# Attention values: full products for the low halves of a head's first queries, and V's largest magnitude taken by halves

## The chip, the cores and the metric

The kernel runs on one core of a Trainium2 chip. The core has a matrix engine (TensorE, PE in the profile; its weight loads are listed apart as PEld), a vector engine (VectorE, DVE), an activation engine (ScalarE, ACT), GpSimd (POOL) and SyncE (SP), whose queue issues the DMA transfers here. Each engine takes its own instructions in the order in which the program has them and waits on semaphores for the others. Operands lie in SBUF, the products' sums in PSUM, which has eight banks of 128 partitions by 512 numbers.

The metric is the device time of one execution in microseconds. A lower time is better.

## What is computed

Two decoder layers over 1024 tokens of width 1024. Layer 0 mixes by causal pooling, layer 1 by a forgetting attention with 16 heads of 64; both have a second, gated branch that attends to 256 memory tokens. The change lies in layer 1:

```python
def shared_kv(x, w_kv_shared, b_forget):
    h = x @ w_kv_shared
    k = h[..., :D_MAIN].reshape(B, S, FOX_HEADS, FOX_HEAD_DIM)
    v = h[..., D_MAIN:2 * D_MAIN].reshape(B, S, FOX_HEADS, FOX_HEAD_DIM)
    log_f = jax.nn.log_sigmoid(h[..., 2 * D_MAIN:] + b_forget)
    return k, v, jnp.cumsum(log_f, axis=1)

def block(args):                                  # 128 queries of forgetting_attention
    logits = jnp.einsum('bqhd,bkhd->bhqk', qi, k) * FOX_HEAD_DIM ** -0.5
    logits = logits + (ci[..., :, None] - cum_k[:, :, None, :])
    logits = jnp.where(mask[None, None], logits, -jnp.inf)       # causal
    p = jax.nn.softmax(logits, axis=-1)
    return jnp.einsum('bhqk,bkhd->bqhd', p, v)
```

## The kernel before

**Precision by halves.** Inputs are float32. An operand is split into a high and a low part, and a product is summed from high x high, low x high and high x low. The attention's probabilities and values are split into two float16 numbers each: `values_of` scales a pair's V by a power of two and `scaled_halves` writes the high half on ACT (L339) and the low half on DVE (L340). The scale comes from the largest magnitude in each of V's 128 rows: L332 reduces 1024 tokens on DVE to one number, L333 keeps it from being zero, L334 to L337 make the scale and its inverse out of its exponent.

**The forgetting attention, `fox`.** It goes through heads `hd` 0 to 15, two to a pair (`pr`), and in a head through eight tiles of 128 queries, from the last (tile 7, 1024 keys) to the first (tile 0, 128 keys). `probs` makes a tile's logits in one or two parts of up to 512 keys, each in one of three L banks (two products, L231). DVE adds the forget gates' row R, takes the row's minimum (the logits are held negated) and empties the bank in one instruction (L986; R was masked on POOL, L978); the second part starts from the first part's minimum. ACT then takes the exponentials into two T banks with the row sums beside them (L994). DVE adds the sums and inverts them (L1004 or L1006, L1007), and a tile later `halves` writes the scaled probabilities as float16 halves, ACT the high one (L1015) and DVE the low one (L1016). A DMA transposes them (L1028).

**`values(hd, c)`.** Once the four tiles of a half of the queries are transposed, PE multiplies them with V: `c = 1` for tiles 7 to 4 (26 blocks of 128 keys), `c = 0` for tiles 3 to 0 (10 blocks). It sums in one bank, O. In L1045 the stationary side is V's high and low half next to each other, 128 columns, so one product gives high V x high P in partitions 0 to 63 and low V x high P in 64 to 127. In L1051 high V alone, 64 columns, meets the low half of P, and blocks go by turns into the upper and the lower half of the array's columns (`128*64` in the profile). At the end ACT and DVE add both halves of the partitions (L1057, L1058).

**Work in between.** While DVE and ACT make the probabilities, PE works through projections in the order of a list (`Fill`): keys, values and queries of the pair after the next, and gates. They go into two pj banks (L253), 24 products of 128x512 a bank and 48 for both halves of the tokens. `chained` sets a pair's order: keys 48, values 24, queries 48, values 24. Each full bank is emptied by ACT and DVE: keys L893 and L894, queries L904 and L905, gates L283 and L284, values by one ACT copy alone (L931) into a tile `u[0]` of 128x1024. When a pair's projections are through, `complete` calls `values_of` on it. The first two pairs get their V in another way (`v_first`), so that `values_of` runs for six.

The order on PE is that of the code. On the other engines a scheduler sets it from its own estimate of times, so an edit can move instructions that it does not name.

Of the kernel before, what the change touches and what calls it, by code (L numbers as in the profile page):

```python
# [9 lines left out]
F32 = mybir.dt.float32  # L10
# [5 lines left out]
ALU = mybir.AluOpType  # L16
AX = mybir.AxisListType

P = 128
# [80 lines left out]
def trunk_kernel(ctx, tc, x, xT, memT, win, wk, wv0, wv, wmk, wmv, wout, poolw, pscale, lng, lnb, bforget, out):  # L100
# [225 lines left out]

    def scaled_halves(u, halves, un, by_tile=lambda t: t):

        m, e, sc = (tiny(1) for _ in range(3))
        nc.vector.tensor_reduce(m, u, AX.X, ALU.max, apply_absolute_value=True)  # L332
        nc.vector.tensor_scalar(m, m, 2.0 ** -100, None, ALU.max)  # L333
        nc.vector.tensor_scalar(e.bitcast(I32), m.bitcast(I32), 0x7F800000, None, ALU.bitwise_and)  # L334
        nc.vector.reciprocal(sc, e)
        nc.vector.tensor_scalar(sc, sc, 2.0 ** 14, None, ALU.mult)
        nc.vector.tensor_scalar(un, e, 2.0 ** -15 / PSCALE, None, ALU.mult)  # L337
        (hi, lo), u = halves, by_tile(u)
        nc.scalar.activation(hi, u, AF.Copy, scale=sc)  # L339
        nc.vector.scalar_tensor_tensor(lo, u, sc, hi, ALU.mult, ALU.subtract)  # L340
# [415 lines left out]
    with tc.tile_pool(name="in1", bufs=1) as in1:  # L756
# [21 lines left out]

        def values_of(u):

            un = unscale[:, len(done) : len(done) + 1]
            done.append(0)
            two = MK([P, ST, 2, P], F16)
            scaled_halves(
                u, [two[:, :, e, :] for e in range(2)], un, lambda t: t.rearrange("p (s t) -> p s t", s=ST),
            )
            v = vt([P, 2, 2 * ST, 64], F16)
            for b in range(2):
                nc.sync.dma_start_transpose(v[:, b, :, :], two[64 * b : 64 * b + 64].rearrange("p s e t -> p (s e t)"))
            return v, un  # L790
# [95 lines left out]
        def pair_units(p):  # L886
# [41 lines left out]
            if p < 2:  # L928
                return keys, queries
            vals = landing(  # L930
                slab(wv[p - 2], XH, XL, lambda cols, acc: nc.scalar.copy(u[0][:, cols], acc)), u, lambda: [MK([P, S], F32)],  # L931
            )
            return chained((keys, 48), (vals, 24), (queries, 48), (vals, 24))

        def complete(p):
            heads, u = pairs[p]
            pairs[p] = list(heads)
            pairs[p].append(first_vs[p] if p < 2 else values_of(u[0]))

# [94 lines left out]
        def values(hd, c, o):  # L1034
# [9 lines left out]
            for n, (i, j) in enumerate(blocks):  # L1044
# [3 lines left out]
                )  # L1048
            for n, (i, j) in enumerate(blocks):
                half = slice(64 * (n % 2), 64 * (n % 2) + 64)  # L1050
# [203 lines left out]
```

## Time and profile before

| what | value |
|---|---|
| median of 3 runs | 1199.49 us (1198.8 to 1199.53) |
| the profiled execution's own time | 1198.79 us |
| its span, first to last instruction | 1197.0 us |
| mean granted TensorE clock | 0.999 |
| layer 1's attention (`fox`), about | 640 to 1075 us |
| PE busy in 640 to 760, 760 to 820, 820 to 860 us | 116.27, 59.17, 38.39 us |
| PE busy in 860 to 925, 925 to 1015, 1015 to 1060 us | 64.07, 86.69, 44.38 us |

A row of the timeline or of the groups names the line of the kernel, the engine, the operation, output and inputs by the program's tile names, and the shapes. A timeline row begins with its start and duration in us and ends, where the engine stood idle before, with that time and what ended it. A group row has the count, the busy time in us, the mean ns of one, and the idle time before. A row of waits has who waited for whom, us in total, how often, and the longest. A row of the windows has the stretch and its length, then the busy time and count on PE and PEld, the granted clock, the share of the DMA engines and GB/s. "issue" is time for which the profile names no releaser.

### The profile page before, as it was taken

What the parts mean: (1) busy time and instruction counts of PE and PEld (TensorE: products, weight loads), DVE (VectorE), ACT (ScalarE), POOL (GpSimd) and SP (SyncE); (2) the same over time, 40 slices, a digit from 0 to 9 for tenths busy, and PEclk for the clock granted to TensorE, in tenths of its full rate; (3) what the DMA queues carried; (4) which work ended last, traced back from release to release, by engine and by line L of the source; (5) the groups of instructions that cost most, each with busy time, mean ns of one, the idle gap of its engine ahead of it and who ended that gap; (6) DMA issues with size and microseconds to landing.
All of it is one profiled execution on the core that took longest, in us unless ns stands there. A gap on an engine that the chain in (4) does not pass through costs nothing. (4 is left out here: it accounts for less than half of the span.)

```text
span 1197.0 us, 19472 instructions
## 1 busy us (share of the span) xinstructions
PE 1172.2 (98%) x6810; PEld 739.3 (62%) x6927; DVE 800.5 (67%) x1864; ACT 616.9 (52%) x1330; POOL 208.4 (17%) x312
## 2 busy tenths in 40 slices
PE   9999999999999999999999999999999999999997
PEld 4567665555555555677776666666666666655554
DVE  6544767374656576377546888778878888874654
ACT  7433654262532224366325777767766787773110
POOL 2000000000000000200103334333334324530000
PEclk9999999999999999999999999999999999999999
DMA  7333654242355666355526789879897999976431
GB/s 246 115 101 87 131 115 159 79 123 80 102 197 158 159 156 161 106 138 100 171 54 161 152 199 173 195 155 195 187 186 164 195 191 210 230 206 229 154 116 48
DMA packets 280803, 182.06 MB, mean 152 GB/s; under 512 B 225024, under 2 KB 238976, under 8 KB 280704
## 3 DMA queue, kind: packets, MB, share of 16 engines
q1 hardware_dynamic: 280704, 180.81, 62.0%
q8 instruction: 54, 0.88, 0.3%
q14 instruction: 45, 0.37, 0.1%
HBM read 95.24 MB, written 22.61 MB: 98 GB/s over the span
## 5 line engine op out<-in xcount | busy, mean ns | idle before, releaser
L253 PE MATMUL pj<-A,w 128*128 128x512 bf16 (+1 forms) x1817 | 571.4, 398 | 2.2 <-DVE B L894 1.1
L253 PE MATMUL pj<-A,wl 128*128 128x512 bf16 x929 | 351.8, 380 | 6.4 <-issue 3.4
L253 PEld LDWEIGHTS pj<-A,w 128*128 128x128 f32 x944 | 174.8, 188 | 45.4 <-POOL wl L200 2.0
L253 PEld LDWEIGHTS <-w 128*128 128x128 bf16 x960 | 93.1, 98 | 121.3 <-issue 39.4
L253 PEld LDWEIGHTS <-wl 128*128 128x128 bf16 x960 | 94.3, 98 | 87.9 <-issue 4.2
L994 ACT ACTIVATE T<-MK,s 128x512 f32<-128x512 f32 x192 | 111.0, 578 | 44.5 <-DVE s L986 22.6
L1015 ACT ACTIVATE P<-T,s 128x512 f16<-128x512 f32 x192 | 103.1, 576 | 52.8 <-issue 26.3
L1016 DVE SCALAR_TENSOR_TENSOR P<-T,s,P 128x512 f16<-128x512 f32 x192 | 112.3, 612 | 24.0 <-ACT P L1015 22.3
L540 PEld LDWEIGHTS <-T 128*128 128x128 bf16 x736 | 70.6, 98 | 88.9 <-issue 6.8
L190 DVE TENSOR_TENSOR wl<-raw,w 128x512 bf16<-128x512 f32 (+1 forms) x96 | 67.9, 713 | 72.3 <-ACT w L189 69.7
L231 PE MATMUL L<-B,B 128*128 128x512 f32 (+3 forms) x384 | 109.0, 386 | 4.6 <-DVE s L986 4.2
L189 ACT CAST w<-raw 128x512 fp32r<-128x512 f32 (+1 forms) x104 | 62.8, 609 | 84.0 <-PE pj L253 57.6
L231 PEld LDWEIGHTS L<-B,B 128*128 128x128 f32 x384 | 71.1, 189 | 29.6 <-DVE s L986 9.9
L353 POOL TENSOR_SCALAR A<-A 128x1024 bf16<-128x1024 f32 x8 | 8.4, 1049 | 444.5 <-ACT A L351 427.9
L986 DVE CUSTOM_DVE_ANT_0 MK<-L,R 128x512 f32<-128x512 f32 (+3 forms) x128 | 72.8, 569 | 8.4 <-PE L L231 5.6
L978 POOL TENSOR_SCALAR_AFFINE_SELECT R<-R 128x128 f32<-128x128 f32 x128 | 42.2, 335 | 207.4 <-DVE s L986 162.5
L200 POOL TENSOR_TENSOR wl<-raw,w 128x512 bf16<-128x512 f32 x54 | 69.4, 1285 | 3.8
L190 DVE TENSOR_TENSOR T<-T,T 128x1024 bf16<-128x1024 f32 x23 | 31.6, 1374 | 48.1 <-ACT T L189 48.0
L189 ACT CAST T<-T 128x1024 fp32r<-128x1024 f32 x23 | 24.1, 1047 | 71.7 <-DMA T<-y1d 45.4
L199 POOL TENSOR_SCALAR w<-raw 128x512 fp32r<-128x512 f32 x54 | 35.9, 665 | 58.5 <-PE pj L253 58.5
L540 PE MATMUL L<-B,T 128*128 128x512 bf16 (+1 forms) x163 | 43.1, 391 | 0.3
L433 ACT ACTIVATE P<-L,s 128x256 f32<-128x256 f32 x64 | 29.6, 474 | 23.4 <-issue 13.0
(296 smaller groups left out, 1789.7 us busy)
## 6 DMA issues: line engine op xcount, KB each, us to landing
raw<-in_win_dram SPq DMA_DIRECT2D x94, 256.0 KB, 2.9
raw<-in_wout_dram SPq DMA_DIRECT2D x40, 256.0 KB, 2.9
B<-B SPq DMA_DIRECT2D x32, 256.0 KB, 4.5
R<-cumd SPq DMA_DIRECT2D x16, 512.0 KB, 4.6
T<-y0d SPq DMA_DIRECT2D x12, 512.0 KB, 5.1
y0d<-Y SPq DMA_DIRECT2D x11, 512.0 KB, 2.7
T<-y1d SPq DMA_DIRECT2D x11, 512.0 KB, 4.7
raw<-in_wmk_dram SPq DMA_DIRECT2D x16, 256.0 KB, 2.7
```

Of the source, the lines that this page charges most:

```text
L189: pin(nc.scalar.copy(hi, src))
L190: pin(by.tensor_tensor(lo[0], src, hi.bitcast(F32), ALU.subtract))
L199: nc.gpsimd.tensor_scalar(hi, src, 1.0, 1.0, ALU.mult, ALU.mult)
L200: nc.gpsimd.tensor_tensor(lo[0], src, hi.bitcast(F32), ALU.subtract)
L231: nc.tensor.matmul(acc, a, b, start=i == 0, stop=i == len(terms) - 1)
L253: nc.tensor.matmul(acc, a, b, start=start, stop=stop)
L540: nc.tensor.matmul(acc, y, w, start=c == 2 and j == firsts[id(acc)] and acc is not self.seeded, stop=c == 1 and j == lasts[id(acc)], skip_ ...
L978: nc.gpsimd.affine_select(R[:, qs], R[:, qs], [[-1, P]], ALU.is_ge, -NEG, base=0, channel_multiplier=1).ins
L986: nc.vector.tensor_tensor_reduce(p[:, lo:up], lg, R[:, lo:up], 1.0, top, ALU.add, ALU.min, m[:, n : n + 1])
L994: nc.scalar.activation(e, p[:, lo:up], AF.Exp, bias=top, scale=-1.0, accum_out=sums[:, n, hd % 2, i : i + 1],)
L1015: nc.scalar.activation(pair[:, lo:up], e, AF.Copy, scale=r)
L1016: nc.vector.scalar_tensor_tensor(pair[:, L + lo : L + up], e, r, pair[:, lo:up], ALU.mult, ALU.subtract)
```

## The change

In `values`, for `c == 0` only, the low half of P meets V's high and low half together, as in L1045, so that ten products of 64 columns become ten of 128 (and low V x low P is added too). For `c == 1` the code is as before. The second part takes V's largest magnitude per half of the tokens: as soon as ACT has copied a half from its bank, DVE reduces these 512 tokens into one column of a small tile `tops`, and `scaled_halves` takes the larger of the two columns where it took a maximum over 1024 tokens.

```diff
-    def scaled_halves(u, halves, un, by_tile=lambda t: t):
+    def scaled_halves(u, halves, un, by_tile=lambda t: t, tops=None):
         m, e, sc = (tiny(1) for _ in range(3))
-        nc.vector.tensor_reduce(m, u, AX.X, ALU.max, apply_absolute_value=True)
-        nc.vector.tensor_scalar(m, m, 2.0 ** -100, None, ALU.max)
+        if tops is None:
+            nc.vector.tensor_reduce(m, u, AX.X, ALU.max, apply_absolute_value=True)
+            nc.vector.tensor_scalar(m, m, 2.0 ** -100, None, ALU.max)
+        else:
+            nc.vector.tensor_scalar(m, tops[:, 0:1], tops[:, 1:2], 2.0 ** -100, ALU.max, ALU.max)
...
+            def v_evac(cols, acc):
+                nc.scalar.copy(u[0][:, cols], acc)
+                n = cols.start // NH
+                nc.vector.tensor_reduce(u[1][:, n : n + 1], u[0][:, cols], AX.X, ALU.max, apply_absolute_value=True)
+
             vals = landing(
-                slab(wv[p - 2], XH, XL, lambda cols, acc: nc.scalar.copy(u[0][:, cols], acc)), u, lambda: [MK([P, S], F32)],
+                slab(wv[p - 2], XH, XL, v_evac), u,
+                lambda: [MK([P, S], F32), small.tile([P, 2], F32, tag="tops", name=nm("tops"), bufs=2)],
             )
...
-            pairs[p].append(first_vs[p] if p < 2 else values_of(u[0]))
+            pairs[p].append(first_vs[p] if p < 2 else values_of(*u))
...
-            for n, (i, j) in enumerate(blocks):
+            if c == 0:
+                for n, (i, j) in enumerate(blocks):
+                    nc.tensor.matmul(
+                        acc[:, cols(i)], v[:, b, 2 * j : 2 * j + 2, :].rearrange("p e d -> p (e d)"),
+                        pt[hd, i][:, i + 1 + j, :], start=False, stop=n == len(blocks) - 1, skip_group_check=True,
+                    )
+            for n, (i, j) in enumerate(blocks if c else ()):
                 half = slice(64 * (n % 2), 64 * (n % 2) + 64)
                 nc.tensor.matmul(
                     acc[half, cols(i)], v[:, b, 2 * j, :], pt[hd, i][:, i + 1 + j, :],
```

Line numbers behind the edits are higher in the changed kernel: L986, L1004, L1007 and L1016 become L996, L1014, L1017 and L1026.

On PE nothing changes its place. The end of the first `values(hd, 0)`, before:

```order
L1051 MATMUL O_6682<-T_6345,V_6084 64x128
L1051 LDWEIGHTS V_6084
L1051 MATMUL O_6682<-T_6376,V_6084 64x128
L253 LDWEIGHTS w_6410
L253 MATMUL pj_6617<-A_3076,w_6410 128x512
L253 LDWEIGHTS wl_6411
```

and now:

```order
L1061 MATMUL O_6682<-T_6345,V_6084 128x128
L1061 LDWEIGHTS V_6084
L1061 MATMUL O_6682<-T_6376,V_6084 128x128
L253 LDWEIGHTS w_6410
L253 MATMUL pj_6617<-A_3076,w_6410 128x512
L253 LDWEIGHTS wl_6411
```

The rows of L1051 have become rows of the new L1061 with 128 columns, and the same projection stands behind them.

On DVE, in head 3 (whose tiles go on while pair 2's first half of V is copied, MK_7111), from the low halves of an earlier tile to the inverse for tile 7, before:

```order
L1016 SCALAR_TENSOR_TENSOR P_7178<-T_7144,s_7175,P_7178 128x256
L986 ISA MK_7196,s_7200<-L_7208,R_6941,s_7200 128x512
L986 ISA s_7200 128x1
L1016 SCALAR_TENSOR_TENSOR P_7212<-T_7181,s_7205,P_7212 128x128
L1004 TENSOR_SCALAR s_7244<-sums_6812 128x1
L986 ISA MK_7235,s_7239<-L_7240,R_6941 128x512
L986 ISA s_7239 128x1
L1007 RECIPROCAL s_7244<-s_7244 128x1
```

and now:

```order
L1026 SCALAR_TENSOR_TENSOR P_7179<-T_7145,s_7176,P_7179 128x256
L937 TENSOR_REDUCE tops_7112<-MK_7111 128x1
L996 ISA MK_7198,s_7202<-L_7210,R_6941,s_7202 128x512
L996 ISA s_7202 128x1
L1026 SCALAR_TENSOR_TENSOR P_7214<-T_7182,s_7207,P_7214 128x128
L996 ISA MK_7237,s_7241<-L_7242,R_6941 128x512
L996 ISA s_7241 128x1
L1014 TENSOR_SCALAR s_7246<-sums_6812 128x1
L996 ISA MK_7237,s_7241<-L_7249,R_6941,s_7241 128x384
L996 ISA s_7241 128x1
L1017 RECIPROCAL s_7246<-s_7246 128x1
```

The reduce of the first half (L937) stands ahead of the second minimum of tile 7; the first minimum of the next tile has gone ahead of L1014, and its second one ahead of L1017.

On DVE, between heads 3 and 4, where `values_of` runs for pair 2, before:

```order
L332 TENSOR_REDUCE s_7556<-MK_7111 128x1
L333 TENSOR_SCALAR s_7556<-s_7556 128x1
L334 TENSOR_SCALAR s_7557<-s_7556 128x1
L335 RECIPROCAL s_7558<-s_7557 128x1
L337 TENSOR_SCALAR unscale<-s_7557 128x1
L1006 TENSOR_SCALAR s_7582<-sums_6812 128x1
L336 TENSOR_SCALAR s_7558<-s_7558 128x1
L1007 RECIPROCAL s_7582<-s_7582 128x1
L986 ISA MK_7573,s_7577<-L_7578,R_7322 128x512
```

and now:

```order
L937 TENSOR_REDUCE tops_7112<-MK_7111 128x1
L336 TENSOR_SCALAR s_7559<-tops_7112 128x1
L337 TENSOR_SCALAR s_7560<-s_7559 128x1
L338 RECIPROCAL s_7561<-s_7560 128x1
L340 TENSOR_SCALAR unscale<-s_7560 128x1
L1016 TENSOR_SCALAR s_7584<-sums_6812 128x1
L339 TENSOR_SCALAR s_7561<-s_7561 128x1
L1017 RECIPROCAL s_7584<-s_7584 128x1
L996 ISA MK_7575,s_7579<-L_7580,R_7324 128x512
```

The place and the count of rows are the same; L937 reduces the second half alone, where L332 reduced both.

More of the change, by code (lines that the diff above doesn't have):

```diff
@@ L777, in trunk_kernel, with values_of @@
             nc.gpsimd.affine_select(later, later, [[1, P]], ALU.not_equal, 1.0, base=-k * HEADS, channel_multiplier=-1)
-        def values_of(u):
+        def values_of(u, tops):
             un = unscale[:, len(done) : len(done) + 1]
@@ L784, in values_of @@
             scaled_halves(
-                u, [two[:, :, e, :] for e in range(2)], un, lambda t: t.rearrange("p (s t) -> p s t", s=ST),
+                u, [two[:, :, e, :] for e in range(2)], un, lambda t: t.rearrange("p (s t) -> p s t", s=ST), tops,
             )
```

## Prediction

> **What bounds the kernel now.** I read the page first, then the groups by line with shapes kept apart, then the waits of TensorE (PE) and of VectorE (DVE) in stretches of the forgetting-attention stage (about 640 to 1060 us), and last the timeline around single calls.
>
> ```profile
> span 1197.0 us, 19472 instructions
> PE 1172.2 (98%) x6810; PEld 739.3 (62%) x6927; DVE 800.5 (67%) x1864; ACT 616.9 (52%) x1330; POOL 208.4 (17%) x312
> PE L L231 <- DVE s L986: 4.2, 9, 1.0
> PE pj L253 <- issue: 3.8, 24, 0.2
> PE pj L253 <- DVE B L894: 1.1, 2, 0.5
> PE pj L253 <- POOL R L978: 0.3, 2, 0.2
> PE pj L253 <- POOL R L1083: 0.2, 1, 0.2
> ```
>
> The last five rows are PE's waits between 640 and 1075 us, but for one of 0.3 us. PE is busy 98% of the span, so a change pays if it takes PE time away or ends one of its waits. Three kinds of wait matter: nine times (4.2 us) PE waits until the row minimum of L986 has emptied one of the three L banks; twice (1.1 us) until L894 has emptied a pj bank; and 24 times it stands for 0.16 us with no releaser ("issue"). The three waits put down to POOL are as long as those and, like them, stand right behind a call of `values`, so I take them for the same thing.
>
> Whether a saving on PE reaches the end depends on who leads. These are DVE's waits, first in 660 to 763 us (six rows), then the one kind in 764 to 805 us that names PE's logits:
>
> ```profile
> DVE P L1016 <- ACT P L1015: 5.7, 10, 1.1
> DVE s L1004 <- ACT T L994: 5.0, 6, 1.3
> DVE s L1006 <- ACT T L994: 1.7, 5, 0.5
> DVE G L1058 <- ACT G L1057: 1.5, 3, 0.9
> DVE MK L986 <- DVE s L986: 0.3, 2, 0.2
> DVE MK L986 <- PE O L1051: 0.2, 1, 0.2
> ...
> DVE MK L986 <- PE L L231: 0.7, 2, 0.4
> ```
>
> From 660 to 763 us DVE never waits for logits: it waits for ScalarE (ACT), ACT for it, and the two set their own pace, with PE running into the full banks. Only after 764 us does DVE wait for PE. The same answers for 805 to 860 and 910 to 1015 us name no logits, that for 860 to 910 us does. So PE leads in some heads and the DVE-ACT chain in the others.
>
> **Full products in `values(hd, 0)`.** One call, the first of sixteen, on PE:
>
> ```profile
> 673.70 0.72 PE L1045 MATMUL O<-T,V 128*128 128x128 f16 x10
> 674.36 0.47 PE L1051 MATMUL O<-T,V 128*64 128x128 f16 x10
> 674.99 0.38 PE L253 MATMUL pj<-A,wl 128*128 128x512 bf16 x1 [0.16 <-issue]
> ```
>
> From the first full product to the projection behind the call: 674.99 - 673.70 = 1.29 us. Ten full ones, then ten half-array ones that run in pairs, then a stand of 0.16 us. The change makes the ten halves full. What a run of full f16 products costs, its exit into the same kind of projection included, stands in the memory attention:
>
> ```profile
> 151.96 0.84 PE L231 MATMUL T<-T,MK 128*128 128x128 f16 x12
> 152.64 0.38 PE L253 MATMUL pj<-A,w 128*128 128x512 bf16 x1
> ```
>
> Twelve products in 0.68 us, 0.057 each, and no stand behind them. Twenty would take 1.13 us, 0.16 less than now. The last call differs, since another product follows it:
>
> ```profile
> 1068.55 0.73 PE L1045 MATMUL O<-T,V 128*128 128x128 f16 x10
> 1069.21 0.47 PE L1051 MATMUL O<-T,V 128*64 128x128 f16 x10
> 1069.61 0.50 PE L540 MATMUL pj<-MK,B 128*128 128x512 f32 x1
> ```
>
> 1.06 us without a stand; it becomes 1.13, so 0.07 longer. Gross: 15 x 0.16 - 0.07 = 2.3 us less on PE. No instruction is added: 320 rows (a weight load and a product each) change shape, and the weights that they load are the pair of halves that L1045 loads already.
>
> A page speaks against this edit. The Trainium skill, "TensorEngine Tiling (Array Packing)", section Theoretical Speedup, promises up to twofold for a stationary side of 64 columns, which is L1051's case; by that alone the halves are the form to keep, and the sum would be that of the second rival below. The same page, section Key Properties, says that a change of the tiling mode drains TensorE, without a price; the stand of 0.16 us behind the halves agrees with it, and for ten products the trace has the drain dearer than the gain.
>
> How much arrives: a call's 0.16 us is lost where PE next runs into the DVE-ACT chain, because it then waits that much longer. I count as kept the calls after which DVE waits for PE, or no such wait of PE follows:
>
> ```profile
> 751.60:753.00 1.40, 0.47 (x10) 0.31 (x10) 1.00 0.91 180
> 780.70:782.10 1.40, 0.47 (x10) 0.31 (x10) 1.00 0.67 207
> 859.50:860.90 1.40, 0.47 (x10) 0.31 (x10) 1.00 0.95 200
> 888.50:889.90 1.40, 0.47 (x10) 0.31 (x10) 1.00 0.88 237
> 1016.20:1017.70 1.50, 0.47 (x10) 0.31 (x10) 1.00 1.13 213
> 1045.30:1046.70 1.40, 0.47 (x10) 0.31 (x10) 1.00 1.48 239
> ```
>
> Six calls (the rows are L1051's ten halves in each): 6 x 0.16 - 0.07 = 0.9 us. Bounds: 0 and 2.3.
>
> **The maximum per half.** It is taken for six pairs of heads. What goes and what stands in for it:
>
> ```profile
> L332 DVE TENSOR_REDUCE s<-MK 128x1 f32<-128x1024 f32 x6 | 7.3, 1216 | 0.0
> L429 DVE TENSOR_REDUCE s<-L 128x2 f32<-128x512 f32 x32 | 20.9, 682 | 0.4 <-PE L L231 0.4
> 734.80 1.22 DVE L332 TENSOR_REDUCE s<-MK 128x1 f32<-128x1024 f32 x1
> 736.82 0.67 DVE L986 CUSTOM_DVE_ANT_0 MK<-L,R 128x512 f32<-128x512 f32 x1
> ```
>
> A half has no row of its own. It lies between 1216 / 2 = 0.61 us and the 0.68 us of L429, which takes 512 elements from a bank; I take 0.65. The tiny maximum of L333 is replaced by one that joins the two halves: nothing. At the pair's end one half is left on DVE ahead of the next head's first minimum (734.80 to 736.82): 1.22 - 0.65 = 0.57 us earlier. The other half is taken 72 products of the pair's projections earlier, and in heads 3, 7, 11 and 13 that is right ahead of the second minimum of the head's first tile:
>
> ```profile
> 710.41 0.58 ACT L931 COPY MK<-pj 128x512 f32<-128x512 f32 x1
> 711.34 0.74 DVE L986 CUSTOM_DVE_ANT_0 MK<-L,R,s 128x512 f32<-128x512 f32 x1
> 712.12 0.69 ACT L994 ACTIVATE T<-MK,s 128x512 f32<-128x512 f32 x1 [0.87 <-DVE s L986]
> 713.68 0.21 DVE L1004 TENSOR_SCALAR s<-sums 128x1 f32<-128x1 f32 x1 [1.33 <-ACT T L994]
> ```
>
> The copy of V from its bank (710.41) is done by then, so the reduce need not wait for it. But ACT waits for that minimum (0.87 us idle), and DVE then for ACT (1.33 us): the reduce takes its 0.65 us ahead of the minimum, not in the idle time behind it. Queued behind it on DVE are the minima of the next tile and all that follows. In the new order the next tile's first minimum goes ahead of L1004, which gives some back, and the inverse, L1007, for which ACT's high halves wait, goes behind its second minimum, which takes some. Per pair the chain therefore ends between 0.57 us earlier (the first half hidden entirely) and 2 x 0.65 - 1.22 = 0.08 later (nothing hidden); I take 0.2 earlier, the middle (0.25) rounded toward the later end because of that inverse. PE runs into the chain behind four of the six ends (heads 4, 8, 12, 14): 4 x 0.2 = 0.8 us, bounds -2.3 to +0.3. The other two lie where PE leads: nothing. The transposing loads of V that hang on this start as much earlier, and PE waits for none of them. On SP and POOL a few R and weight transfers change places with a transpose; PE's waits name no DMA, and POOL only in the three rows above, so I take nothing.
>
> **Sum.** 0.9 + 0.8 = 1.7 us less. The profiled execution took 1198.79 us, 1.8 more than its span, and becomes 1197.1; the median of the runs, 1199.49, lies 0.7 above it and becomes 1197.8. That is 0.14%, inside the 0.2% (2.4 us) that a measurement of this kernel can tell from no change.
>
> **Rivals.**
> *The whole of it arrives.* The DVE-ACT chain may follow PE more closely than its waits say (its evictions of pj and O start when PE is done). Then 2.3 us of products count, and half of the largest gain of the maxima (4 x 0.57 / 2 = 1.1): 1196.1. For it: PE is busy 98%. Against it: the six rows of DVE's waits.
>
> *The halves were the faster form* (slower). By busy time they are:
>
> ```profile
> L1045 PE MATMUL O<-T,V 128*128 128x128 f16 x576 | 37.4, 219 | 0.0
> L1051 PE MATMUL O<-T,V 128*64 128x128 f16 x576 | 22.2, 222 | 0.0
> ```
>
> 37.4 / 576 against 22.2 / 576 is 65 against 39 ns a product; 160 products times 26 ns is +4.2 us, 1203.7, if the stand of 0.16 us is not theirs but the projection's, and stays behind full products. (The Trainium skill's rule of the twofold speedup would have it so.) Against it: the memory attention's exit has no stand. It decides if the 27 stands remain.
>
> *The first half lengthens the chain* (slower). If nothing of 4 x 0.65 us is hidden and the gain at the pair's end is eaten by ACT, which is then late: 2.6 - 0.9 = +1.7, 1201.2; if the reduce also waits out a copy of V from its bank, (the 0.58 us row), 4 x 0.58 = 2.3 more, 1203.5. It decides from the first minimum that starts late enough to fill the third L bank; the idle 1.33 us speaks against it, the row order for it.
>
> **How the numbers follow.** Forecast 0.50; all arrives 0.33; halves faster 0.07; chain longer 0.10. Faster by over 0.2% means under 1197.1: the 0.33 and 0.03 of the forecast's edge, 0.36. Slower means over 1201.9: 0.07 and 0.06 of the last case, 0.13. Within: 0.51. The forecast's own range is 1196.9 to 1199.2; for 8 in 10 it reaches down into the first rival, nearly to both low bounds together (1199.5 - 2.3 - 2.3 = 1194.9), and up to the shorter price of the last: 1195.0 to 1201.0.
>
> **What would show it.** Right: L1051 left with 416 products; about 12 stands of 0.16 us on PE, those behind `values(hd, 1)`, in place of 27 (24 "issue" and three POOL); the twenty full products within 1.13 us; new reduces of about 0.65 us, twelve of them; PE's waits for L986 grown by some tenths of a us in heads 2, 7, 11, and shrunk at heads 4, 8, 12, 14. Wrong: still 27 stands (they are not the halves'), or PE's waits for DVE unchanged with the whole 2.3 us gone from the span (the chain does follow PE), or waits for L986 of a us each in heads 3, 7, 11, 13 (the first half is not hidden).

## The result, and the profile after

The kernel became slower. Five runs of each on one chip:

| | before | after |
|---|---|---|
| median of 5 runs, us | 1199.49 | 1203.85 (1203.23 to 1204.72) |
| ratio, with 95% interval | | 1.0039 [1.0029, 1.005] |
| the profiled execution's own time, us | 1198.79 | 1203.23 |
| its span, us | 1197.0 | 1201.4 |

The forecast was 1197.8 us, with a range of 1195.0 to 1201.0. So the sign was wrong, and the time lies outside the range.

The page of the changed kernel, its span and the busy times (share of the span, number of instructions):

```profile
span 1201.4 us, 19476 instructions
PE 1174.5 (98%) x6810; PEld 743.1 (62%) x6927; DVE 802.5 (67%) x1870; ACT 615.7 (51%) x1330; POOL 207.6 (17%) x312
```

PE's recorded busy time is 2.3 us longer than before (1172.2), DVE's 2.0, and the span 4.4. PE's waits between 640 and 1075 us, the same view as before (line numbers have moved by ten: L996 is L986 of before, L1055 is L1045, L1061 the new full products and L1067 what is left of L1051):

```profile
PE L L231 <- DVE s L996: 7.5, 11, 1.5
PE pj L253 <- issue: 1.9, 12, 0.2
PE pj L253 <- DVE B L897: 1.1, 2, 0.6
```

Two things changed. The stands for "issue" went from 24 to 12, as the prediction asked for, and PE's waits for the row minimum went from 4.2 to 7.5 us, which it did not. They grew at heads 4, 8, 12 and 14 too (0.60, 0.58, 1.46 and 0.59 us, the longest at each, in the timelines), where they were to shrink. The reduces of the second edit are a group of their own on DVE:

```profile
L937 DVE TENSOR_REDUCE tops<-MK 128x1 f32<-128x512 f32 x12 | 8.2, 681 | 1.1 <-ACT MK L935 1.1
```

0.68 us each, at the upper end of the bounds (0.61 to 0.68), and 1.1 us of waiting for V's copy, which the reduce of before did not have (0.0 in its row).

**Where the 4.4 us arise.** From both timelines I took the start of the first row minimum (L986, after: L996) of each head and subtracted. The third column is a kernel of the experiments below, the change with no other instruction moved:

| first minimum of head | 2 | 3 | 4 | 5 | 6 | 7 | 8 | 9 | 10 | 11 | 12 | 13 | 14 | 15 |
|---|---|---|---|---|---|---|---|---|---|---|---|---|---|---|
| after - before, us | -0.11 | 0.55 | 1.02 | 1.27 | 1.94 | 1.92 | 2.40 | 2.68 | 3.37 | 3.35 | 3.81 | 3.76 | 4.20 | 4.19 |
| p_after - before, us | 0.15 | 0.15 | 0.27 | 0.62 | 0.38 | 0.37 | 0.49 | 0.90 | 0.69 | 0.69 | 0.80 | 0.79 | 1.08 | 1.08 |

The changed kernel slips in three kinds of places: 0.66 us in head 2, where no reduce stands yet; about 0.47 us from head 3 to 4, 7 to 8, 11 to 12 and 13 to 14; and about 0.9 us from head 4 to 6 and from 8 to 10.

### The profile page after: what moved, and what is told of

It reads as the page before. It is cut to its first block, busy times and chain, and to the rows that moved or that the text cites. A ratio compares the mean times of both kernels' runs of the same rounds, so it can differ in the third digit from the quotient of the medians.

```text
span 1201.4 us, 19476 instructions
## 1 busy us (share of the span) xinstructions
PE 1174.5 (98%) x6810; PEld 743.1 (62%) x6927; DVE 802.5 (67%) x1870; ACT 615.7 (51%) x1330; POOL 207.6 (17%) x312
## 5 line engine op out<-in xcount | busy, mean ns | idle before, releaser
L1025 ACT ACTIVATE P<-T,s 128x512 f16<-128x512 f32 x192 | 102.9, 577 | 62.6 <-issue 33.9
L1004 ACT ACTIVATE T<-MK,s 128x512 f32<-128x512 f32 x192 | 110.9, 578 | 43.8 <-DVE s L996 24.8
L1026 DVE SCALAR_TENSOR_TENSOR P<-T,s,P 128x512 f16<-128x512 f32 x192 | 111.8, 613 | 31.8 <-ACT P L1025 30.3
L996 DVE CUSTOM_DVE_ANT_0 MK<-L,R 128x512 f32<-128x512 f32 (+3 forms) x128 | 72.7, 568 | 7.5 <-PE L L231 4.2
```

Of the source, the lines that this page charges most:

```text
L996: nc.vector.tensor_tensor_reduce(p[:, lo:up], lg, R[:, lo:up], 1.0, top, ALU.add, ALU.min, m[:, n : n + 1])
L1004: nc.scalar.activation(e, p[:, lo:up], AF.Exp, bias=top, scale=-1.0, accum_out=sums[:, n, hd % 2, i : i + 1],)
L1025: nc.scalar.activation(pair[:, lo:up], e, AF.Copy, scale=r)
L1026: nc.vector.scalar_tensor_tensor(pair[:, L + lo : L + up], e, r, pair[:, lo:up], ALU.mult, ALU.subtract)
```

## Experiments

Each was timed against the kernel before on the same chip, in five rounds on four chips. Kernels of different rounds are compared by what each differs from its own before. Medians are of 5 to 11 runs, those of before of 21 to 33.

| run | what | median, us | before, us | ratio, 95% interval |
|---|---|---|---|---|
| e_products | full products alone | 1201.69 | 1199.27 | 1.0023 [1.0014, 1.0033] |
| e_maxima | maxima per half alone | 1202.75 | 1199.27 | 1.0032 [1.002, 1.0044] |
| e_joined | two halves, both at the pair's end in the code | 1200.36 | 1199.27 | 1.0011 [1.0002, 1.002] |
| e_tiny | first half's reduce cut to 8 tokens | 1200.70 | 1199.27 | 1.0014 [1.0005, 1.0023] |
| p_products | full products, order of before | 1199.22 | 1198.93 | 1.0003 [0.9994, 1.0012] |
| p_ahead | maxima, order of before, first half ahead | 1199.88 | 1198.93 | 1.001 [1.0001, 1.0018] |
| p_after | both edits, order of before | 1199.99 | 1198.93 | 1.001 [1.0001, 1.0019] |
| p_behind | maxima, order of before, first half behind | 1197.90 | 1198.93 | 0.999 [0.9982, 0.9999] |
| p_inverse | kernel before, four rows moved | 1202.45 | 1198.93 | 1.0032 [1.0021, 1.0044] |
| p_evict | kernel before, four other rows moved | 1200.29 | 1198.93 | 1.0011 [1.0002, 1.0021] |
| p_best1 | p_behind, first half one place later | 1197.49 | 1198.93 | 0.9989 [0.998, 0.9997] |
| p_best2 | p_best1, V's scale behind the next minima | 1194.97 | 1198.93 | 0.9967 [0.9955, 0.998] |
| a_inverse | after, four rows moved | 1201.87 | 1198.99 | 1.0023 [1.0014, 1.0032] |
| a_inverses | after, eight rows moved | 1200.26 | 1198.99 | 1.0012 [1.0003, 1.0021] |
| a_tile6 | after, second tile's rows as before | 1202.76 | 1199.19 | 1.0028 [1.0018, 1.0039] |
| a_reduce | after, two reduces in the old place | 1202.02 | 1199.19 | 1.0022 [1.0012, 1.0032] |
| a_both | both of these | 1200.68 | 1199.19 | 1.0012 [1.0003, 1.0021] |

### The two parts apart

e_products keeps `scaled_halves`, `values_of` and `pair_units` of before; e_maxima keeps `values` of before. In e_joined the code of the reduces moves into `values_of`; in e_tiny the first one is cut:

```diff
             def v_evac(cols, acc):
                 nc.scalar.copy(u[0][:, cols], acc)
                 n = cols.start // NH
-                nc.vector.tensor_reduce(u[1][:, n : n + 1], u[0][:, cols], AX.X, ALU.max, apply_absolute_value=True)
+                some = cols if n else slice(0, 8)
+                nc.vector.tensor_reduce(u[1][:, n : n + 1], u[0][:, some], AX.X, ALU.max, apply_absolute_value=True)
```

e_products:

> Only the first part of the change: the ten low-half products of values(hd, 0) are full ones, V's maximum stays one reduce over 1024 tokens. Theory A (recount: the 0.16 us stand behind the halves is no stand but a product of 512 columns, 216 ns, whose record is missing; a call then costs 1.065 us before and 1.116 us now): 16 x 0.05 = +0.8 us, 1200.3 us, give or take half a us for DVE instructions that the scheduler moves in heads 2 and 3. Theory B (my prediction: a stand of 0.16 us goes): -0.9 to -2.3 us, 1197.2 to 1198.6. Theory C (halves at the price of their busy time): +4.2 us, 1203.7.

e_maxima:

> Only the second part: V's maximum per half of the tokens, with the 64-column products kept. Theory A (most of the loss lies in the chain of DVE and ACT, which the first half's reduce and the instructions moved with it lengthen): +3 to +3.6 us, 1202.5 to 1203.1 us, with PE waits of 0.4 to 0.8 us in heads 3, 7 and 11. Theory B (my prediction): -0.8 us, 1198.7. Theory C (all of the loss is the products'): within 0.5 us of before.

e_joined:

> 64-column products; the maximum is taken per half, but both reduces stand at the pair's end, where the one reduce stood. It costs DVE 1.36 instead of 1.22 us there. Theory A1 (the place of the first half, in the middle of a head, makes the loss): 4 x 0.14 = +0.6 us at most, 1199.5 to 1200.1. Theory A2 (not the place but the instructions that the scheduler moves whenever the DVE work of a pair's end changes, make it): over +1.5 us, 1201.0 or more.

e_tiny:

> As the second part of the change alone, but the first half's reduce reads 8 of its 512 tokens, so that 504 tokens are left out of the magnitude. It stands in the same place, behind the same copy, and takes about 0.1 instead of 0.68 us. Theory A1 (the 0.68 us of DVE time in the middle of a head make the loss): the gain of 0.54 us at four pair ends is left, about -1.5 us, 1198.0. Theory A2 (the moved instructions, and the wait for the copy): it loses nearly as much as the whole second part, 1201.5 to 1203.

Measured against before: +2.4, +3.5, +1.1 and +1.4 us. None of my theories gave +2.4 for the products, and the two parts together (5.9) are more than the change (4.4), so they are not simple terms of a sum. e_joined and e_tiny lie between their theories and settle nothing by themselves.

What the four have in common is the scheduler. Each is a new program to it, and it moved rows that the edit does not name. By the traces, at least 21 of DVE's rows stand in another order in e_products, 22 in e_joined and in e_tiny, 52 in e_maxima and 63 in the change itself (the fewest rows whose moving makes one order of the other, rows of one name taken as the same and the edit's own left out). In e_joined, which has its reduces later in the code, it put the first one behind the second minimum of the head's first tile on its own, where e_maxima has it ahead. So the next runs took the scheduler out.

### The order held fixed

A table holds the place of every instruction of DVE, ACT, POOL and SP in the kernel before, and a helper lays it over another kernel as edges of issue order, which add no wait. A new instruction is put next to a named one:

```diff
+EXTRAS, MINIMA = {}, {}
+FIRST = {p: ((2 * p - 1, 7, 1), 1) for p in (2, 4, 6, 7)} | {p: ((2 * p - 2, 1, 0), 1) for p in (3, 5)}
...
         trunk_kernel(tc, *args)
+        in_order(nc, tc, EXTRAS)
```

FIRST names, for each pair p, the minimum (head, tile, part) at which the first half's reduce stands, behind it (1) or ahead of it (0: p_ahead, p_after). The second half's reduce takes the place of L332. p_products needs no such row. Rows other than these stand as before on all four engines, and PE's order is the code's: in p_products' trace not one row of DVE, ACT, POOL or SP has another place than before. No run has the table over the kernel before itself; p_products is the nearest to it.

p_products:

> Full products in values(hd, 0) alone, with every instruction of DVE, ACT, POOL and SP queued in the order of the kernel before (the products-only run of the first round had 115 DVE rows moved and cost +2.4 us). Theory A (recount of the products, +0.05 us a call; all else of the +2.4 is the moved rows): 16 x 0.05 = +0.8 us, 1200.1 us. Theory A' (the wider products themselves make DVE late, not the moved rows): still +2 us or more, 1201.3. Theory B (prediction): -0.9 to -2.3 us.

p_ahead:

> As the run before it, but the first half's reduce right ahead of the second minimum in heads 3, 7, 11 and 13, as the change has it; everything else in the order of the kernel before. Theory A1 with the place as its cause: the chain pays 0.68 us and gets 0.54 back, 4 x 0.14 = +0.6 us, 1199.9; if the place is the whole of the loss, +3.5 us, 1202.8. Theory A2 (the moved rows, not the place, make the +3.5 of the second part alone): -0.5 to +0.6 us.

p_after:

> The whole change with no row moved but its own: full products and the first half's reduce ahead of the second minimum, all else in the order of the kernel before. Theory A (edits +0.8 and +0.6, the rest of the +4.4 us is the scheduler's moves): +1.4 us, 1200.7. Theory A' (the edits themselves cost it all): +4 us, 1203.3.

p_behind:

> 64-column products, maximum per half; DVE, ACT, POOL and SP in the order of the kernel before, the second half's reduce in the place of the old one, and the first half's reduce right behind the second minimum of the first tile in heads 3, 7, 11 and 13 (behind the first minimum of tile 1 in heads 4 and 8 for the other two pairs), where DVE waits for ACT anyway. Theory A1 (place and moved rows make the loss; the split itself gains at the pair's end): 4 x (0.44 to 0.54) = -1.8 to -2.2 us, 1197.1 to 1197.5. Rival (a first half costs its 0.68 us wherever it stands): +0.6 us, 1199.9.

The products cost +0.3 us, which is no change that can be measured; the reduce ahead of the minimum +0.95; both together +1.1. The change cost +4.4, so about 3.3 us of it came from rows that the scheduler moved. And the same reduce behind the minimum is 1.0 us faster than before: not the 1.8 that I expected, but the sign of A1.

**The products, read in these runs.** The first call of `values(hd, 0)` in p_behind, which still has the 64-column products (L1062 and L1068 are L1045 and L1051 there), from PE's timeline:

```profile
673.68 0.72 PE L1062 MATMUL O<-T,V 128*128 128x128 f16 x10
674.33 0.47 PE L1068 MATMUL O<-T,V 128*64 128x128 f16 x10
674.73 0.39 PE L253 MATMUL pj<-A,w 128*128 128x512 bf16 x1
674.96 0.38 PE L253 MATMUL pj<-A,wl 128*128 128x512 bf16 x1
```

And the same place in p_products:

```profile
674.87 0.72 PE L1045 MATMUL O<-T,V 128*128 128x128 f16 x10
675.42 0.72 PE L1051 MATMUL O<-T,V 128*128 128x128 f16 x10
675.98 0.38 PE L253 MATMUL pj<-A,w 128*128 128x512 bf16 x1
676.20 0.38 PE L253 MATMUL pj<-A,wl 128*128 128x512 bf16 x1
```

In p_behind a product with `w` stands right behind the halves, 0.23 us ahead of the one with `wl`. In the trace of before the first record behind the call is the one with `wl`, as far from the call's start as here (674.96 - 673.68 = 1.28; before 674.99 - 673.70 = 1.29). In that of after it is `wl` too, 1.33 us from the start as in p_products (676.20 - 674.87). The product with `w` stands between in the program's order, but has no record, and what it took looked like a stand of 0.16 us. The pages say as much. First p_behind, then p_products:

```profile
PE 1180.4 (99%) x6927; PEld 739.5 (62%) x6927; DVE 801.2 (67%) x1870; ACT 616.3 (52%) x1330; POOL 207.9 (17%) x312
```

```profile
PE 1182.6 (99%) x6927; PEld 743.4 (62%) x6927; DVE 800.9 (67%) x1864; ACT 616.8 (51%) x1330; POOL 207.9 (17%) x312
```

Here every one of the 6927 weight loads has its product. The traces of before and after have 6810 products, 117 too few. In the executions of p_behind and p_products the waits of PE between 640 and 1075 us hold no row for "issue" at all, with the halves or without; p_inverse, below, which has the kernel's own halves, has the 24 again. So the stands came and went with the recording, not with the products.

From first product to the next one outside the call, p_behind takes 674.73 - 673.68 = 1.05 us and p_products 675.98 - 674.87 = 1.11. Full products cost 0.06 us more a call, not 0.16 less; to the second projection it is 0.05 (1.33 against 1.28), so 0.8 to 1.0 us for sixteen. The median moved by 0.3, which its interval does not tell from nothing: in the timelines a call shifts PE by 0.05 to 0.06 us, and where DVE and ACT lead (heads 2, 3, 4, 7, 8 and 11 to 14) the next wait swallows it.

**The maxima, read in these runs.** With the order held, a reduce ahead of the minimum puts the head's chain 0.59 us back (p_ahead, DVE's starts in heads 3, 7 and 11), and the pair's end gives 0.48 back, so +0.11 a pair. (The row lasts 0.68 us, but the next one starts 0.59 behind its start. Four pairs make 0.44; the median's +0.95 has an interval from 0.1 to 2.2 us.) Behind the minimum it costs 0.14 and the end gives the same 0.48. From DVE's and ACT's timeline of p_behind in head 3 (L1001 is L986, L788 the reduce, L1011 the exponential, L1021 the sum):

```profile
711.31 0.74 DVE L1001 CUSTOM_DVE_ANT_0 MK<-L,R,s 128x512 f32<-128x512 f32 x1
...
711.98 0.68 DVE L788 TENSOR_REDUCE tops<-MK 128x1 f32<-128x512 f32 x1
...
712.10 0.69 ACT L1011 ACTIVATE T<-MK,s 128x512 f32<-128x512 f32 x1 [0.87 <-DVE s L1001]
...
713.80 0.21 DVE L1021 TENSOR_SCALAR s<-sums 128x1 f32<-128x1 f32 x1 [0.88 <-ACT T L1011]
```

ACT starts at 712.10, 0.02 us earlier than before (712.12), though the reduce takes its 0.68 us: it fills DVE's wait for ACT, which shrinks from 1.33 to 0.88 us. What is left, 0.14 us, goes with the low half (L1016 of before, 128x128) that now stands behind it, and for which ACT's next exponential waits; in p_best1 below, where the reduce stands behind that low half, the 0.14 us are gone.

### Which moved rows cost so much

First, single rows moved in the kernel before. p_inverse: the reciprocal in `inverse_of` (L1007) for tile 7 of heads 3, 7, 11 and 13, behind the second minimum of tile 6. p_evict: the eviction at the end of `values(hd, 0)` (L1058), behind the low halves of tile 4 of the next head:

```diff
-            nc.vector.reciprocal(r, r)
+            made = nc.vector.reciprocal(r, r).ins
+            if i == 7 and hd in (3, 7, 11, 13):
+                MOVED[made.name] = made, (hd, 6, 1), 1
             return r
```

> The kernel before, no edit in its computation; four DVE rows moved by hand: in heads 3, 7, 11 and 13 the inverse of the first tile's row sums (the reciprocal) stands behind the next tile's second minimum instead of ahead of it, as the scheduler put it in the run of the second part alone. ACT's high halves of the first tile wait for that inverse. Theory A2 (moved rows are most of the loss; the second part alone lost some 0.46 us a pair more than the run with the reduce ahead and nothing else moved): 4 x 0.46 = +1.8 us, 1200.8. Rival (the chain has slack there): +0.2 us or less.

> The kernel before, no edit in its computation; four DVE rows moved by hand: in heads 3, 7, 11 and 13 the eviction of O behind values(hd, 0) of the head before (the last step of values) stands behind the two low halves of tile 4 instead of ahead of them, as the scheduler put it in the run of the products alone, where each pair's end came 0.35 us later. Theory A2 (that row alone did it): 4 x 0.35 = +1.4 us, 1200.4. Rival (the inverse that moved beside it did it): +0.3 us or less.

+3.5 and +1.4 us. Neither kernel computes anything else than before, or in another way: four rows of 0.16 us each, moved past one 0.62 us minimum, cost 3.5 us. p_inverse in head 3 (L1009 is the inverse, L1019 and L1020 the high and low halves):

```profile
714.63 0.62 DVE L986 CUSTOM_DVE_ANT_0 MK<-L,R,s 128x384 f32<-128x384 f32 x1 [0.17 <-DVE s L986]
715.18 0.16 DVE L1009 RECIPROCAL s<-s 128x1 f32<-128x1 f32 x1
715.42 1.26 ACT L1019 ACTIVATE P<-T,s 128x512 f16<-128x512 f32 x2 [1.81 <-issue]
716.14 1.41 DVE L1020 SCALAR_TENSOR_TENSOR P<-T,s,P 128x512 f16<-128x512 f32 x2 [0.81 <-ACT P L1019]
```

And the kernel before at the same place:

```profile
714.42 0.16 DVE L1007 RECIPROCAL s<-s 128x1 f32<-128x1 f32 x1
714.66 1.27 ACT L1015 ACTIVATE P<-T,s 128x512 f16<-128x512 f32 x2 [1.01 <-issue]
...
715.38 1.41 DVE L1016 SCALAR_TENSOR_TENSOR P<-T,s,P 128x512 f16<-128x512 f32 x2
```

The inverse comes 0.76 us later, the high halves 0.76, the low halves 0.76, and nothing behind them catches up: each head's chain keeps 0.80 us of it, four heads 3.2. DVE and ACT hand each tile to and fro here, and while one waits for the other every delay on that path is the pair's time.

Then the rows of the changed kernel itself, its own order held and some of its rows moved. First I took the inverses, since they had cost so much:

> The changed kernel with its own order on every engine, but for four DVE rows: in heads 3, 7, 11 and 13 the inverse of the first tile's row sums goes back ahead of the next tile's second minimum, where the kernel before has it. Theory A2 (these rows are most of what the scheduler's moves cost): the +4.4 us of the change fall to what its edits cost, +1.1 us, or to about +2 us where other moved rows keep a part: 1200.0 to 1201.3. Rival (the other moved rows cost it): 1203 or more.

> As a_inverse, with the inverse of the second tile's row sums also put back ahead of the third tile's second minimum in these heads. If the rule is the same for each tile, 0.1 to 0.5 us less for each of four heads than a_inverse: 0.4 to 2 us less. If DVE's chain has caught up by then: the same as a_inverse.

They are 2.9 and 1.3 us slower than their own before, so 1.5 and 3.1 less than the changed kernel's 4.4. That repairs most of it, but it does not find the cause: between the first tile's sum and its inverse stands one minimum in the changed kernel, and one before too (another one), so that a_inverse, with none between them, makes an order better than that of before. In the timelines the first minimum slips by 0.01 to 0.04 us from head 3 to 4, 7 to 8, 11 to 12 and 13 to 14, less than the reduce alone costs (0.11), and in a_inverses it gains 0.37 to 0.39. The expectation for a_inverse took it for the order of before.

What differs in the changed kernel is the second tile. Its rows in head 3 (L1004 the exponentials, L1073 and L1074 the two evictions of O, L996 the minima, L1014 and L1017 sum and inverse, L1025 the high halves):

```profile
718.11 0.69 ACT L1073 ACTIVATE G<-O,unscale 64x512 f32<-64x512 f32 x1
718.70 0.57 ACT L1004 ACTIVATE T<-MK,s 128x384 f32<-128x384 f32 x1
718.83 0.74 DVE L1074 SCALAR_TENSOR_TENSOR G<-O,unscale,G 64x512 f32<-64x512 f32 x1 [0.94 <-ACT G L1073]
719.50 0.67 DVE L996 CUSTOM_DVE_ANT_0 MK<-L,R 128x512 f32<-128x512 f32 x1
720.10 0.20 DVE L1014 TENSOR_SCALAR s<-sums 128x1 f32<-128x1 f32 x1
720.35 0.48 DVE L996 CUSTOM_DVE_ANT_0 MK<-L,R,s 128x256 f32<-128x256 f32 x1
720.76 0.16 DVE L1017 RECIPROCAL s<-s 128x1 f32<-128x1 f32 x1
721.00 1.16 ACT L1025 ACTIVATE P<-T,s 128x512 f16<-128x512 f32 x2 [1.61 <-issue]
```

And before:

```profile
716.89 0.56 ACT L994 ACTIVATE T<-MK,s 128x384 f32<-128x384 f32 x1
717.60 0.69 ACT L1057 ACTIVATE G<-O,unscale 64x512 f32<-64x512 f32 x1
717.61 0.21 DVE L1004 TENSOR_SCALAR s<-sums 128x1 f32<-128x1 f32 x1 [0.82 <-ACT T L994]
717.86 0.16 DVE L1007 RECIPROCAL s<-s 128x1 f32<-128x1 f32 x1
718.32 1.16 ACT L1015 ACTIVATE P<-T,s 128x512 f16<-128x512 f32 x2
```

Before, the second exponential runs ahead of O's eviction, and sum and inverse stand right behind it. After, ACT evicts O first, and DVE takes an eviction and two minima ahead of the inverse. The high halves start 2.68 us later than before, where the first tile's (715.76 against 714.66 in the timelines) were 1.10 late, and the head 0.55 at its start.

The other place is head 5, and head 9 likewise. Before, the one reduce stood 7 us behind the copy of V (780.59, 0.57 us long); after, the second half's stands right behind it, and has to wait for it. After, then before:

```profile
782.46 0.69 DVE L937 TENSOR_REDUCE tops<-MK 128x1 f32<-128x512 f32 x1 [0.54 <-ACT MK L935]
```

```profile
788.18 1.21 DVE L332 TENSOR_REDUCE s<-MK 128x1 f32<-128x1024 f32 x1
```

DVE stands 0.54 us and then spends 0.68, with the sums and inverses of the next tiles behind it. a_tile6 puts back the rows of the second tile, a_reduce the reduce of heads 5 and 9, a_both both:

> The changed kernel in its own order, but for the rows of the second tile of heads 3, 7, 11 and 13, as the kernel before has them: on DVE the sum and the inverse of its row sums ahead of the eviction of O and the next two minima, on ACT its second exponential ahead of the eviction of O. If these rows are what the four pairs lose beyond the reduce: 4 x (0.47 - 0.11) = 1.4 us less than the changed kernel, 1202.4. If other rows do it: within 0.5 us of it, 1203.4 or more.

> The changed kernel in its own order, but in heads 5 and 9 the second half's reduce stands where the kernel before has its one reduce, some 7 us behind V's copy, instead of right behind the copy, for which DVE there waits 0.54 us before it spends 0.68 on it. If that is the loss in heads 5/6 and 9/10: 2 x 0.8 = 1.6 us less than the changed kernel, 1202.2. If the slip comes from elsewhere: within 0.5 us of it.

> Both of them. If the two causes are right and add up: 3.0 us less than the changed kernel, 1200.8, which leaves the edits' own +1.1 and head 2's +0.66. If they stand in for each other: no more than the larger of the two.

They are 3.6, 2.8 and 1.5 us slower than their own before, so 0.8, 1.5 and 2.9 less than the changed kernel's 4.4, where 1.4, 1.6 and 3.0 were expected. The medians alone do not tell whether the two add up; the timelines do. From head 0 to head 15 the first minimum slips by 4.39 us in the changed kernel, 3.13 in a_tile6, 2.75 in a_reduce and 1.33 in a_both: 1.3 and 1.6 less, and 3.1 for both, so both are causes. Each acts where it should: the four slips of 0.47 become 0.11 to 0.14 in a_tile6, what the reduce costs with nothing else moved, and those from head 4 to 8 and from 8 to 12 fall from 1.37 and 1.41 to 0.48 and 0.53 in a_reduce.

What a_both has left, +1.5 us, is near the edits' own +1.1, but head 2's slip of 0.66 us is still in it (from 0.74 to 1.42 us between the first minima of heads 2 and 3). That slip is in e_products and not in e_maxima, and no run undid it alone. Its place can be read in the timeline of after (L897 empties the bank of the keys, L894 before):

```profile
699.39 0.21 DVE L1014 TENSOR_SCALAR s<-sums 128x1 f32<-128x1 f32 x1
699.65 0.48 DVE L996 CUSTOM_DVE_ANT_0 MK<-L,R,s 128x256 f32<-128x256 f32 x1
700.17 0.69 DVE L897 TENSOR_TENSOR B<-pj,B 64x512 fp32r<-64x512 f32 x1
700.90 0.16 DVE L1017 RECIPROCAL s<-s 128x1 f32<-128x1 f32 x1
```

And before:

```profile
698.97 0.69 DVE L894 TENSOR_TENSOR B<-pj,B 64x512 fp32r<-64x512 f32 x1
699.69 0.48 DVE L986 CUSTOM_DVE_ANT_0 MK<-L,R,s 128x256 f32<-128x256 f32 x1
700.10 0.21 DVE L1004 TENSOR_SCALAR s<-sums 128x1 f32<-128x1 f32 x1
700.34 0.16 DVE L1007 RECIPROCAL s<-s 128x1 f32<-128x1 f32 x1
```

After, the eviction stands between sum and inverse. The minimum ahead of it is 0.04 us early, the inverse 0.56 late, and the head keeps that. This is read, not tested.

### A version faster than both

The reduce behind the minimum was already 1.0 us faster than before. p_best1 moves it behind one more row, the low half of the previous head's last tile. p_best2 moves the rest of V's scale as well, for the four pair's ends where DVE leads: the second reduce and the five small rows behind it to behind the next head's first two minima, V's high half (L339) behind that tile's exponentials, V's low half (L340) behind its inverse, V's loads behind the last transpose of the head before. For these pairs `values_of` is also called later in the code, and the scale's small numbers get buffers of their own. A part of the diff:

```diff
+            for i in (where, top, one, two, three, four):
+                MOVED[i.name] = i, at, 1
+                at = i.name
+            MOVED[high.name] = high, ("exp", 2 * pair, 7, 1), 1
+            MOVED[low.name] = low, ("inverse", 2 * pair, 7), 1
```

> As the run with the first half's reduce behind the second minimum (1.03 us faster than before), but the reduce behind the low half of the previous head's last tile as well, where the scheduler had it in the run with both reduces at the pair's end. There DVE then has nothing else to do until ACT's exponentials are through. If the 0.14 us that the reduce still cost in each of four heads goes: 4 x 0.14 = 0.6 us more, -1.6 us against before, 1197.3. If the reduce costs its 0.14 us in either place: -1.0 us.

> As p_best1, and at the ends of the four pairs where DVE leads (heads 4, 8, 12, 14) the second half's reduce and the scale behind it stand behind the next head's first two minima, V's high half on ACT behind that tile's exponentials, V's low half behind that tile's inverse, and V's two transposing loads behind the last tile's transpose. If the pair's end is what makes PE wait there (its waits on DVE in those four heads come to some 3.4 us, and p_best1 takes 1.9 of them): up to 1.5 us less than p_best1, -3 us against before, 1196. If V is then late for its products, or DVE only waits elsewhere: not faster than p_best1.

1197.49 and 1194.97 us: 1.4 and 4.0 us faster than before. In p_best2 the head that follows starts its first minimum ahead of V's scale (L1028 the minima, L799 the reduce, L1038 the exponential):

```profile
735.05 0.67 DVE L1028 CUSTOM_DVE_ANT_0 MK<-L,R 128x512 f32<-128x512 f32 x1
...
735.90 0.75 DVE L1028 CUSTOM_DVE_ANT_0 MK<-L,R,s 128x512 f32<-128x512 f32 x1 [0.17 <-DVE s L1028]
...
736.58 0.68 DVE L799 TENSOR_REDUCE tops<-MK 128x1 f32<-128x512 f32 x1
736.70 0.69 ACT L1038 ACTIVATE T<-MK,s 128x512 f32<-128x512 f32 x1 [1.11 <-DVE s L1028]
```

Before, that minimum started at 736.82, behind the reduce and its scale. PE's waits for the minima between 640 and 1075 us fall from nine times, 4.2 us, to:

```profile
PE L L231 <- DVE s L1028: 3.1, 5, 0.9
```

Each of the four pair's ends gave about 0.9 us (DVE's starts against before: 0.06 in head 3, -0.89 in head 6; -0.89 and -1.80 around head 8).

## Why the prediction was wrong, point by point

- **"a stand of 0.16 us" and "Twenty would take 1.13 us, 0.16 less than now".** This step failed. The stand is a product without a record, 117 of which are missing from that trace. Twenty full products took 1.11 us, as forecast, but the 1.29 us that I held against them contained a projection: the halves take 1.05. The term "15 x 0.16 - 0.07 = 2.3 us" was 0.8 to 1.0 us the other way. The forecast kept 0.9 us of a gain; measured was +0.3, no change that can be told. Nor was the stand a sign of a drain, for which the prediction took it. My check of the exit (the memory attention, without a stand) compared a place with a complete record with one without.
- **The sign that was to show it.** 24 stands became 12 and L1051 was left with 416 products, both as forecast, and no time was gained: in the changed kernel's trace the missing product leaves 0.05 us, too little for the view. The first sign of being wrong, 27 stands that remain, could not come for the same reason. A sign that the recording can make says nothing of the cause.
- **The rival "halves were the faster form".** It gave 1203.7 and the kernel took 1203.85, which is luck: a half is shorter by 28 ns between the changes of form (next section but one), near the rival's 26, but the changes take most of that back, so that a call is only 0.06 us shorter, and the rival's +4.2 us of products measured +0.3. The Trainium skill, "TensorEngine Tiling (Array Packing)", Theoretical Speedup, promises up to twofold; the trace agrees for a product between the changes (0.028 against 0.056 us), but the whole call gained 5%, 1.05 against 1.11 us. Its Key Properties say that a change of the mode drains TensorE, and the runs agree: 0.10 us are lost on the way in and 0.12 on the way out.
- **"A half ... I take 0.65", "0.57 us earlier" at the pair's end.** Near: the reduce lasts 0.68, and the end gives 0.48.
- **"Per pair the chain therefore ends between 0.57 us earlier ... and 0.08 later ... I take 0.2 earlier".** The case was just past the later bound: +0.11 a pair with the reduce ahead and nothing else moved, and p_ahead +0.95 us in all where 0.8 less was forecast. The step that failed is the idle time that was to hide a part. The row order that I quoted for the rival spoke truer than the idle time behind it: 1.33 us of waiting behind a minimum hid nothing of a reduce that stood ahead of it.
- **"rounded toward the later end because of that inverse".** This is the step that cost most. I saw that the scheduler moves other rows, priced the inverse at 0.05 us a pair, and left the rest of the moved rows, the eviction of O and the second tile's inverse among them, without a price. The inverse that I priced cost nothing beyond the reduce (its high halves are 0.55 us later than their head, the reduce takes 0.59); the others made about 3.3 of the 4.4 us. Of that a_both took back 2.9, at the second tiles (0.8 by a_tile6's median, 1.3 in its timeline) and where a reduce came to wait for its copy in heads 5 and 9 (1.5 and 1.6 by a_reduce); the rest, by difference, lies in head 2. With nothing moved (p_after, +1.1) the sign would still have been wrong, for the two steps above.
- **"The other two lie where PE leads: nothing".** Right for the edit alone: in p_ahead the first minimum is 0.22 us late in head 4 and 0.21 in head 6. Wrong in the order that the scheduler made: from head 4 to 6 and from 8 to 10 the changed kernel lost about 0.9 us each, where a reduce that waits for its copy used up DVE's idle time.
- **"It decides from the first minimum that starts late enough to fill the third L bank".** The rival of the longer chain had the right place: the chain is where the time went, and its chance was 0.10. But by itself the reduce in the chain is +0.95 us, not 1.7. Its longer price, 1203.5, is close to 1203.85 by luck: it has a reduce wait for its copy in four heads, and the waits came in two others (heads 5 and 9, 1.1 us in all). The sign that it hung on, waits of a us each in heads 3, 7, 11 and 13, came in part: 0.77, 0.77, 0.76 and none.

## What to carry to other kernels

Before a short idle time behind a burst of products is taken for a stand, compare the number of products with the number of weight loads on the page, and the first row behind the gap with the program's order. Where two engines hand a tile to and fro, price every row that the new order moves past another, however short: its own time says little, what waits for it decides (here 0.16 us rows that cost 0.8 each). And when an edit comes out slower under a scheduler, hold the old order fixed and run the edit again, before the edit is judged: here the same reduce was worth +0.95 or -1.4 us by its place alone.

## What the runs showed of the hardware that was not expected

A change between full and 64-column products costs time at both ends. Ten full products take 0.55 us ahead of full ones (675.42 - 674.87) and 0.65 ahead of halves (674.33 - 673.68): 0.10 us for entering. The ten halves and the way out take 0.40 (674.73 - 674.33), ten full ones 0.56 (675.98 - 675.42). The way out can be told apart by `values(hd, 1)`, which p_behind has 10 us earlier, with 26 products of each form:

```profile
663.62 1.61 PE L1062 MATMUL O<-T,V 128*128 128x128 f16 x26
665.16 0.92 PE L1068 MATMUL O<-T,V 128*64 128x128 f16 x26
666.01 0.39 PE L253 MATMUL pj<-A,w 128*128 128x512 bf16 x1
```

Twenty-six halves and the way out take 0.85 us (666.01 - 665.16), ten take 0.40: sixteen more cost 0.45, so 0.028 each, half of a full product's 0.056. Ten halves are 0.28 of the 0.40 us, and the way out is 0.12. So halves save 0.28 us on ten products, entering and leaving cost 0.22, and 0.06 is left. By these numbers the two forms would be even at about eight products between two changes (an estimate). The Trainium skill ("TensorEngine Tiling (Array Packing)", Key Properties) has the drain, without a price.

The number of recorded products differs between executions of nearly the same program, 6810 (before, after, p_inverse) or 6927 (p_products, p_behind), while all 6927 weight loads are there in each.
